# Two-layer hybrid decoder on one core: the two norms after each projection rewritten (gain at the eviction, squares from the bank, sums in groups), and a bank of its own for the last block

## The chip, the cores and the metric

The kernel runs on one core of a Trainium2 chip. The time is device microseconds of one launch. Inside the core five engines work side by side, each through its own queue in order: TensorE (PE in the profile: matrix products; PEld is its loading of weights), VectorE (DVE), ScalarE (ACT), GpSimd (POOL) and SyncE (SP, which here only issues DMAs). An instruction that waits holds up everything behind it in its engine's queue.

The kernel before takes 1241.69 us (median of 3 runs, 1241.63 to 1242.22).

## The reference, cut to what matters

Sequence 512 plus 16 learned tokens ahead of it (L = 528), model width D = 1024, two layers, all float32. The two lines that the change touches are the two sandwich norms:

```python
def _rmsnorm(x, w):
    y = x * lax.rsqrt(jnp.mean(x * x, axis=-1, keepdims=True) + EPS)
    return y * w

for i in range(DEPTH):                                       # 2
    m = mixer(_rmsnorm(h, pre_mix_norm[i]), ...)             # one projection, two attention-like groups, w_out
    h = h + _rmsnorm(m, post_mix_norm[i])
    f = conv_ffn(_rmsnorm(h, pre_ffn_norm[i]), ...)          # ffn_up, conv of width 3, gelu * gate, ffn_down
    h = h + _rmsnorm(f, post_ffn_norm[i])
return h[:, N_META:]
```

So after each of the four products (w_out and ffn_down, in each layer) comes a pair of norms: the product's result is normalised, weighted and added to h, and the new h is normalised and weighted for the next product. After the last ffn_down there is only the first of the pair.

## The kernel before

**Layout.** h and everything that enters a product lie with features on the 128 partitions and tokens along the free dimension: 8 tiles of 128 features, 528 tokens. Tokens go in two halves, 0 to 232 and 232 to 528 (in layer 1 the first half is 14 to 232, 218 tokens, behind the mixer). A float32 product is made of three 16-bit ones: weight and input are split into a high and a low 16-bit part, and `product_step` issues high·high (L469), high·low (L470: low part of the input) and low·high (L471: low part of the weight) for each tile. The weights come by DMA (SP queue) into `st`, ACT makes their high part (L120) and DVE the low part (L124), both into `unit`, just ahead of use.

**A product and its norms.** In `out_proj` (banks `po`) and `ffn_down` (`pd`) the first half's 8 output tiles are computed, then the second half's 8, then the next product (`pu` of ffn_up, or `pj` of the next mixer) starts with the first half's tokens. Each output bank is copied to `m` by ACT (L1106, L1298), squared by ACT from `m` (L430 or L433), and the square is added to `acc` (L435: in `out_proj` on GpSimd except for the last tile, in `ffn_down` on DVE). A half's `norms` (L438) then runs in steps that the kernel lays between the matmuls of what follows: `token_rstd` brings the sum over partitions (a matmul into `nst`, L419), a multiply-add on DVE (L402), the power -1/2 on GpSimd (L403), and spreads the result over all partitions by a matmul with a diagonal (`ndg` L647, `nbc` L643). Then for each of the 8 tiles: DVE m·gain·rstd into `tmp` (L448), GpSimd h += tmp (L450), ACT the square of h (L430/L433), DVE its addition (L435); a second `token_rstd`; and `scaled`: for each tile DVE h·gain·rstd into `tmp` (L656), ACT the high part (L407), DVE the low part (L408), into the input `xh` of the next product.

**What sets the order.** The kernel's beginning is ordered by hand; everything behind it is put in order by a scheduler that works from a cost table of its own, so an edit in one place can move instructions of other places in the queues.

**The seams.** The first half's norms run beside the second half's matmuls; the second half's norms run beside the next product's first matmuls. A seam is a place where PE turns to a half whose `xh` has only just been made: S1 (layer 0, w_out to ffn_up, about 279 us, needs the first half's), S2 (in layer 1's mixer, about 660 us, where its first-half projection is over and the second half's `xh`, from layer 0's ffn_down, is needed), S3 (layer 1, w_out to ffn_up, about 895 us, needs the first half's).

**The end.** `last_down` computes the last product with tokens on partitions, in four blocks of 128 tokens, by a scheme with fewer products than usual; the last block's last piece ("t4", block 3) is done in two column halves of 256, both into bank `pa[1]`. Each half is squared (L1392) and weighted (L1396) from the bank; then the last sum (L1397), the power (GpSimd, L1398), four results of 256 columns (L1401) and their DMAs (L1402).

Of the kernel before, what the change touches and what calls it, by code (L numbers as in the profile page):

```python
# [126 lines left out]
class Quarter:  # L127
# [22 lines left out]
    def fetch(self):  # L150
# [17 lines left out]
        nc.vector.scalar_tensor_tensor(out=self.unit[:, 1], in0=x, scalar=SW, in1=self.unit[:, 0], op0=ALU.mult, op1=ALU.subtract)  # L168
# [48 lines left out]
class Kern:  # L217
# [112 lines left out]
    def constants(self):  # L330
        nc, a, c = self.nc, self.a, self.const
        widths = (("h", KD * L), ("xroom", KD * L), ("ident", P), ("ones", P), ("mhalf", 10), ("par", NROW), ("pars", 48), ("cvec", 4 * 88), ("ss", 10), ("first", 10),
# [33 lines left out]
    def gains(self):  # L366
# [8 lines left out]
        nc.vector.tensor_scalar(out=self.pars[:, 16:], in0=pt[:, :32], scalar1=SX, scalar2=None, op0=ALU.mult)  # L375
# [61 lines left out]
    def norms(self, m, acc, xh, n0, n1, rpost, rpre):  # L437
# [6 lines left out]
        bc = out[0]  # L444
        acc2 = self.sm([P, WN], "acc", bufs=4)
        for k in range(KD):
            t = self.sm([P, WN], "tmp")
            nc.vector.scalar_tensor_tensor(out=t[:, :n], in0=m[:, k, n0:n1], scalar=self.par[:, rpost + k : rpost + k + 1],  # L448
                                           in1=bc[:, :n], op0=ALU.mult, op1=ALU.mult)
            nc.gpsimd.tensor_tensor(out=self.h[:, k, n0:n1], in0=self.h[:, k, n0:n1], in1=t[:, :n], op=ALU.add)  # L450
# [198 lines left out]

    def scaled(self, bc, xh, n0, n1, rpre):  # L650

        nc = self.nc
        n = n1 - n0
        for k in range(KD):
            t = self.sm([P, WN], "tmp")
            nc.vector.scalar_tensor_tensor(out=t[:, :n], in0=self.h[:, k, n0:n1], scalar=self.pars[:, rpre + k : rpre + k + 1],  # L656
                                           in1=bc[:, :n], op0=ALU.mult, op1=ALU.mult)
            self.split(xh[k], t[:, :n], n0, n1)
            if k % 2:
                yield  # L660
# [431 lines left out]
    def out_proj(self, l):  # L1092
# [7 lines left out]
        for n0, n1 in self.halves(l):  # L1100
            acc = self.sm([P, WN], "acc", bufs=4)
            for ct in range(KD):
# [3 lines left out]
                nc.scalar.activation(m[:, ct, n0:n1], ps[:, : n1 - n0], AF.Copy, scale=IW)  # L1106
                self.sumsq(acc, ct, m[:, ct, n0:n1], n1 - n0, ct == KD - 1)
                self.tick()
            gens.append(self.norms(m, acc, xh, n0, n1, R_POST + 8 * l, R_PREF + 8 * l))
# [4 lines left out]
    def input_sums(self):  # L1114

        nc = self.nc
        xf = cell(self.keep, [P, KD, L], F32, "xf", "xf", 1)
# [164 lines left out]
    def ffn_down(self, l, av):  # L1282
# [6 lines left out]
        for g in range(2):  # L1289
            for half, (n0, n1) in enumerate(hv):  # L1290
                for ct in range(4 * g, 4 * g + 4):
# [6 lines left out]
                    nc.scalar.activation(m[:, ct, n0:n1], ps[:, : n1 - n0], AF.Copy, scale=IAW)  # L1298
                    self.sumsq(accs[half], ct, m[:, ct, n0:n1], n1 - n0, True)
                    self.tick()  # L1300
                if g == 1:
                    gens.append(self.norms(m, accs[half], xh, n0, n1, R_POSTF + 8 * l, R_PRE + 8 * (l + 1)))
                    self.finish(gens[-1])
# [3 lines left out]
    def last_down(self, l, av):  # L1307
# [39 lines left out]
        def final(t):  # L1347
            s = self.sm([P, 2], "sst")[:, :1]
            nc.vector.tensor_tensor(out=s, in0=ss[:, 2 * t : 2 * t + 1], in1=ss[:, 2 * t + 1 : 2 * t + 2], op=ALU.add)
            r = self.rstd(s, 1, 1.0 / D, EPS)  # L1350
            for i in range(2):
# [122 lines left out]
```

## Time and profile before

| | |
|---|---|
| median of the runs | 1241.69 us |
| the profiled execution | 1243.79 us |
| its span, first to last recorded instruction | 1241.7 us |
| PE busy | 1221.0 us (98%) |
| DVE busy | 838.9 us (68%) |
| ACT busy | 667.5 us (54%) |
| GpSimd busy | 160.0 us (13%) |
| granted PE clock, mean | 0.998 |
| PE's share of the chain that ended last | 90% |

The profile is of one execution. A row of the timeline reads: start in us from the span's start, duration in us, engine, line, operation, output<-input, tile size, how many in a row ("x2"), and in brackets the engine's idle time before it with what ended it. Matmuls overlap in the pipe: the start of one to the start of the next is what a matmul costs, not its duration. A row of the windows reads: window and its length, then busy us (and instruction count) of PE, PEld, DVE, ACT and POOL, the granted PE clock as a share of full speed, the share of DMA time, and GB/s. In a group, "16 instructions" stands as x16, followed by the group's busy us and the mean ns of one.

### The profile page before, as it was taken

The page shows a single profiled execution, that of the slowest core. Times are in us where ns is not written, and L with a number is a line of the kernel's source. Part 1 is how long each engine was busy: PE and PEld are TensorE (multiplying, and loading weights), DVE is VectorE, ACT ScalarE, POOL GpSimd, SP SyncE. Part 2 cuts the span into 40 slices and gives each one's busy share as a digit, 9 for nine tenths or more (in the row PEclk, how much of TensorE's full clock was granted, in tenths as well). Part 3 has the DMA queues.
Part 4 walks back from the last instruction along what each step waited for, and adds up shares of the span by engine and source line. Part 5 has one row for each costly group of instructions (what it writes and reads, how often), then busy time and mean ns, then how long its engine had stood idle before and what let it go on. Part 6 is the DMA issues. An engine that isn't in the chain of part 4 may idle for free.

```text
span 1241.7 us, 26411 instructions
## 1 busy us (share of the span) xinstructions
PE 1221.0 (98%) x11079; PEld 1013.5 (82%) x11079; DVE 838.9 (68%) x1485; ACT 667.5 (54%) x1316; POOL 160.0 (13%) x205
## 2 busy tenths in 40 slices
PE   8999999999999999999999999999999999999997
PEld 7778888988888888988887788889798888886444
DVE  5677745467998777623465777443769768887686
ACT  5674445454776666523335654453648556664442
POOL 1012311153000000000220223011520000000001
PEclk9999999999999999999999999999999999999999
DMA  7932121131423333424243232212314333304461
GB/s 202 273 102 86 60 79 52 52 97 40 136 70 110 100 97 96 119 73 108 63 114 98 69 86 70 69 52 69 104 51 136 102 103 103 119 2 170 160 239 68
DMA packets 207275, 124.18 MB, mean 100 GB/s; under 512 B 6880, under 2 KB 194836, under 8 KB 207156
## 3 DMA queue, kind: packets, MB, share of 16 engines
q1 hardware_dynamic: 206708, 121.71, 33.7%
q8 instruction: 87, 1.43, 0.5%
q0 software_dynamic: 160, 0.52, 0.1%
q14 instruction: 32, 0.26, 0.1%
q10 hardware_dynamic: 288, 0.26, 0.1%
HBM read 120.38 MB, written 2.10 MB: 99 GB/s over the span
## 4 chain that ended last, share of the span: by engine, by line
PE 90%; ACT 3%; DVE 3%; issue 1%; POOL 1%; DMA 0%; SPq 0%; POOLq 0%; DVEq 0%; ACTq 0%
PE pu L470 11%; PE pu L471 11%; PE pu L469 11%; PE pl L1324 8%; PE pj L469 7%; PE pj L471 7%; PE pj L470 7%; PE pp L1145 3%; PE pd L470 3%; PE pd L471 3%; PE pd L469 3%; PE po L469 2%; PE po L471 2%; PE po L470 2%; PE o L776 1%
## 5 line engine op out<-in xcount | busy, mean ns | idle before, releaser
L470 PE MATMUL pu<-every,unit 128*128 128x296 f16 (+2 forms) x1248 | 341.2, 274 | 2.1 <-DVE every L408 2.1
L471 PE MATMUL pu<-every,unit 128*128 128x296 f16 (+2 forms) x1248 | 341.2, 274 | 0.0
L469 PE MATMUL pu<-every,unit 128*128 128x296 f16 (+2 forms) x1248 | 339.6, 274 | 0.7 <-ACT every L407 0.7
L471 PEld LDWEIGHTS <-unit 128*128 128x128 f16 x2700 | 264.4, 98 | 44.2 <-issue 3.8
L469 PEld LDWEIGHTS <-unit 128*128 128x128 f16 x2700 | 264.6, 98 | 43.9 <-issue 3.9
L470 PEld LDWEIGHTS <-unit 128*128 128x128 f16 x2700 | 264.8, 98 | 39.0 <-issue 0.6
L124 DVE SCALAR_TENSOR_TENSOR unit<-st,unit 128x1024 f16<-128x1024 f32 (+1 forms) x173 | 212.0, 1227 | 100.7 <-ACT unit L120 100.0
L471 PE MATMUL pj<-every,unit 128*128 128x296 f16 (+2 forms) x888 | 244.8, 276 | 0.9 <-DVE unit L124 0.9
L469 PE MATMUL pj<-every,unit 128*128 128x296 f16 (+2 forms) x888 | 245.1, 276 | 0.5 <-DVE room L933 0.5
L470 PE MATMUL pj<-every,unit 128*128 128x296 f16 (+2 forms) x888 | 244.9, 276 | 0.0
L120 ACT ACTIVATE unit<-st 128x1024 f16<-128x1024 f32 (+1 forms) x171 | 177.9, 1041 | 75.1 <-PE pu L471 21.2
L1201 ACT ACTIVATE u<-pu 128x296 f32<-128x296 f32 (+2 forms) x156 | 58.5, 378 | 72.6 <-PE pu L471 72.6
L435 DVE TENSOR_TENSOR acc<-acc,sq 128x296 f32<-128x296 f32 (+2 forms) x60 | 33.4, 558 | 77.6 <-ACT sq L433 75.7
L471 PE MATMUL pd<-av,unit 128*128 128x232 f16 (+1 forms) x308 | 84.7, 276 | 0.0
L470 PE MATMUL pd<-av,unit 128*128 128x232 f16 (+1 forms) x308 | 84.7, 276 | 0.0
L469 PE MATMUL pd<-av,unit 128*128 128x296 f16 (+1 forms) x308 | 84.5, 276 | 0.0
L403 POOL TENSOR_TENSOR every<-every 128x5 f32<-128x5 f32 (+6 forms) x31 | 38.1, 1229 | 295.7 <-DVE every L402 250.4
L1324 PE MATMUL pl<-unit,fk 128*128 128x512 f16 x330 | 71.4, 379 | 0.0
L1190 DVE SCALAR_TENSOR_TENSOR cg<-u,every,cg 128x527 f32<-128x527 f32 (+1 forms) x88 | 66.4, 754 | 5.0 <-ACT cg L1185 4.3
L471 PE MATMUL po<-merged,unit 128*128 128x296 f16 (+2 forms) x256 | 69.7, 274 | 0.0
L470 PE MATMUL po<-merged,unit 128*128 128x296 f16 (+2 forms) x256 | 69.7, 274 | 0.0
L469 PE MATMUL po<-merged,unit 128*128 128x296 f16 (+2 forms) x256 | 69.4, 274 | 0.0
(260 smaller groups left out, 1745.7 us busy)
## 6 DMA issues: line engine op xcount, KB each, us to landing
st<-in_ffn_up SPq DMA_DIRECT2D x78, 512.0 KB, 3.8
st<-in_w_in SPq DMA_DIRECT2D x56, 512.0 KB, 4.6
st<-in_ffn_down SPq DMA_DIRECT2D x46, 512.0 KB, 3.9
st<-in_w_out SPq DMA_DIRECT2D x16, 512.0 KB, 3.6
st<-in_ffn_up SPq DMA_DIRECT2D x20, 256.0 KB, 4.0
st<-in_ffn_down SPq DMA_DIRECT2D x8, 384.0 KB, 3.4
xt<-in_x SPq DMA_DIRECT2D x6, 256.0 KB, 6.2
w<-in_ffn_down SPq DMA_DIRECT2D x3, 512.0 KB, 4.3
```

What stands on the lines that cost most here:

```text
L120: self.kern.nc.scalar.activation(self.u[:, 0], self.st, AF.Copy, scale=SW)
L124: self.kern.nc.vector.scalar_tensor_tensor(out=self.u[:, 1, ks], in0=self.st[:, ks], scalar=SW, in1=self.u[:, 0, ks], op0=ALU.mult, op1=AL ...
L403: nc.gpsimd.tensor_tensor(out=r[:w, :n], in0=t[:w, :n], in1=self.mhalf[:w, :n], op=ALU.pow)
L435: eng.tensor_tensor(out=acc[:, :n], in0=acc[:, :n], in1=sq[:, :n], op=ALU.add)
L469: nc.tensor.matmul(ps[:, :n], w[:, 0, kk, :], x[:, 0, n0:n1], start=first, stop=False)
L470: nc.tensor.matmul(ps[:, :n], w[:, 0, kk, :], x[:, 1, n0:n1], start=False, stop=False)
L471: nc.tensor.matmul(ps[:, :n], w[:, 1, kk, :], x[:, 0, n0:n1], start=False, stop=last)
L776: nc.tensor.matmul(o[:, i, :], intra(i), vn(i), start=i == 0, stop=i == 0, skip_group_check=i > 0)
L1145: mm = lambda p, q, **kw: nc.tensor.matmul(ps, u[:, p, k, :], x[k][:, q], skip_group_check=more, **kw)
L1190: nc.vector.scalar_tensor_tensor(out=to, in0=u[:, max(lo, d) - d : L - d], scalar=self.cvec[:, ci(i) : ci(i) + 1], in1=to, op0=ALU.mult, o ...
L1201: nc.scalar.activation(u[:, n0:n1], ps[:, : n1 - n0], AF.Copy, scale=IXW)
L1324: mm = lambda x, w, **kw: nc.tensor.matmul(ps[:, cols], x, w[:, cols], skip_group_check=more, **kw)
```

## The change

`gained` takes the place of copy and `sumsq`: ACT's copy out of the bank now also multiplies with the norm weight (a scale per partition, from the widened table `pars`), and the square is taken from the bank itself, with a scalar scale. Who adds the squares is as before.

`norms` works in groups of tiles instead of tile by tile. First pass, groups of 4, 2 and 2: one DVE multiply of `m` by the spread rstd, one DVE addition to h (GpSimd before), one ACT square into `m`, and DVE additions that fold the group into `acc2`. Second pass, groups of 2, 2 and 4: one DVE multiply h·rstd into `m` (L468), then for each tile ACT the high part with the weight as scale (L471) and DVE the low part (L472). `scaled` is gone.

In `last_down` block 3's first 256 columns of "t4" go to a bank of their own, `pe`; what earlier pieces had left in `pa[1]` for those columns is copied out ahead (`done`, L1384) and added by DVE (L1399). The other blocks' results (L1356) come after the last weights' low part (L168) on DVE. The last sum is made before the second half is weighted, and the last row of results goes out in three pieces (512, 256, 256 columns).

```diff
-    def sumsq(self, acc, k, src, n, last):
+    def gained(self, ps, out, rpost, acc, k, n, scale, last):
+        nc.scalar.activation(out, ps, AF.Copy, scale=self.pars[:, rpost + k : rpost + k + 1])
         if k == 0:
-            nc.scalar.activation(acc[:, :n], src, AF.Square)
+            nc.scalar.activation(acc[:, :n], ps, AF.Square, scale=scale)
         else:
             sq = self.sm([P, WN], "sq", bufs=3)
-            nc.scalar.activation(sq[:, :n], src, AF.Square)
+            nc.scalar.activation(sq[:, :n], ps, AF.Square, scale=scale)
             eng = nc.vector if last else nc.gpsimd
             eng.tensor_tensor(out=acc[:, :n], in0=acc[:, :n], in1=sq[:, :n], op=ALU.add)
...
     def norms(...)
-        for k in range(KD):
-            t = self.sm([P, WN], "tmp")
-            nc.vector.scalar_tensor_tensor(out=t[:, :n], in0=m[:, k, n0:n1], scalar=self.par[:, rpost + k : rpost + k + 1],
-                                           in1=bc[:, :n], op0=ALU.mult, op1=ALU.mult)
-            nc.gpsimd.tensor_tensor(out=self.h[:, k, n0:n1], in0=self.h[:, k, n0:n1], in1=t[:, :n], op=ALU.add)
-            self.sumsq(acc2, k, self.h[:, k, n0:n1], n, True)
-            if k in (3, 6):
-                yield
-        yield
+        add = lambda to, x, y: nc.vector.tensor_tensor(out=to, in0=x, in1=y, op=ALU.add)
+        spread = lambda bc, k: bc[:, None, :n].to_broadcast([P, k, n])
+        for k0, k1 in ((0, 4), (4, 6), (6, 8)):
+            mk, hk = m[:, k0:k1, n0:n1], self.h[:, k0:k1, n0:n1]
+            nc.vector.tensor_tensor(out=mk, in0=mk, in1=spread(out[0], k1 - k0), op=ALU.mult)
+            add(hk, hk, mk)
+            nc.scalar.activation(mk, hk, AF.Square)
+            if k1 - k0 == 4:
+                add(mk[:, :2], mk[:, :2], mk[:, 2:])
+            if k0 == 0:
+                add(acc2[:, :n], mk[:, 0], mk[:, 1])
+            else:
+                add(mk[:, 0], mk[:, 0], mk[:, 1])
+                add(acc2[:, :n], acc2[:, :n], mk[:, 0])
+            yield
         yield from self.token_rstd(acc2, n0, n1, out)
-        yield from self.scaled(out[1], xh, n0, n1, rpre)
+        for k0, k1 in ((0, 2), (2, 4), (4, 8)):
+            mk = m[:, k0:k1, n0:n1]
+            nc.vector.tensor_tensor(out=mk, in0=self.h[:, k0:k1, n0:n1], in1=spread(out[1], k1 - k0), op=ALU.mult)
+            for k in range(k0, k1):
+                gain = self.pars[:, rpre + k : rpre + k + 1]
+                nc.scalar.activation(xh[k][:, 0, n0:n1], mk[:, k - k0], AF.Copy, scale=gain)
+                nc.vector.scalar_tensor_tensor(out=xh[k][:, 1, n0:n1], in0=mk[:, k - k0], scalar=gain, in1=xh[k][:, 0, n0:n1], op0=ALU.mult, op1=ALU.subtract)
+            yield
...
     def last_down(...)
+        done = self.g([P, 512], F32, "part")[:, :256]
+        nc.scalar.activation(done, pa[1][:, :256], AF.Copy, scale=IAW)
+        pe = self.mm([P, 512], "pl")
...
-        for i, cols in enumerate(half):
-            multiply(("t4", av["x22"], {1: pa[1]}, True), cols=cols)
...
+        multiply(("t4", av["x22"], {1: pe}, False), cols=first)
+        nc.vector.scalar_tensor_tensor(out=y[0][:, first], in0=pe[:, first], scalar=IAW, in1=done, op0=ALU.mult, op1=ALU.add)
...
+        multiply(("t4", av["x22"], {1: pa[1]}, True), cols=last)
...
+        for i, c0, n in ((1, 0, 512), (0, 0, 256), (0, 256, 256)):
```

How the queues read. A row is line, operation, output<-input, tile and the semaphores it waits for (DMAHW is a weight load that landed, Activation is ACT).

DVE at seam S1 before, from the low part of a weight unit (L124) that stands ahead of the second pass of the first half's norms:

```order
L124 SCALAR_TENSOR_TENSOR unit<-st,unit 128x1024 [waits DMAHW2_49,Activation_49]
L656 SCALAR_TENSOR_TENSOR tmp<-every,nbc 128x232 [waits PE_49]
L656 SCALAR_TENSOR_TENSOR tmp<-every,nbc 128x232 x3
L408 TENSOR_TENSOR every<-tmp,every 128x232 [waits Activation_49] x2
L656 SCALAR_TENSOR_TENSOR tmp<-every,nbc 128x232 [waits DVE_49]
L656 SCALAR_TENSOR_TENSOR tmp<-every,nbc 128x232
L124 SCALAR_TENSOR_TENSOR unit<-st,unit 128x1024 [waits DMAHW3_49,PE_49,Activation_49]
L408 TENSOR_TENSOR every<-tmp,every 128x232 [waits Activation_49] x2
```

The same stretch of DVE's queue after the change:

```order
L124 SCALAR_TENSOR_TENSOR unit<-st,unit 128x1024 [waits DMAHW2_49,Activation_49]
L468 TENSOR_TENSOR m<-every,nbc 128x2x232 [waits PE_49]
L468 TENSOR_TENSOR m<-every,nbc 128x2x232
L468 TENSOR_TENSOR m<-every,nbc 128x4x232 [waits DVE_49]
L440 TENSOR_TENSOR acc<-acc,sq 128x296 [waits Activation_49,Pool_49]
L124 SCALAR_TENSOR_TENSOR unit<-st,unit 128x1024 [waits DMAHW3_49,PE_49,Activation_49]
L472 SCALAR_TENSOR_TENSOR every<-m,every 128x232 [waits Activation_49] x5
```

The first low part of `xh` (L408 before, L472 after; `every` holds `xh`) stood behind four single-tile products; it now stands behind all eight tiles' products, the second half's last addition (L440) and a unit's low part. S3 has the same order with 218 tokens.

ACT at S1 before, from the copy of the second half's last bank but one:

```order
L1106 ACTIVATE m<-po 128x296
L433 ACTIVATE sq<-m 128x296 [waits Activation_49]
L407 ACTIVATE every<-tmp 128x232 [waits DVE_49] x2
L1106 ACTIVATE m<-po 128x296 [waits PE_49]
L120 ACTIVATE unit<-st 128x1024 [waits DMAHW3_49]
L407 ACTIVATE every<-tmp 128x232 [waits DVE_49] x2
L433 ACTIVATE sq<-m 128x296 [waits Activation_49]
```

And ACT there after the change, from the last bank:

```order
L433 ACTIVATE m<-po,every 128x296 [waits PE_49]
L438 ACTIVATE sq<-po 128x296
L120 ACTIVATE unit<-st 128x1024 [waits DMAHW3_49]
L471 ACTIVATE every<-m,every 128x232 [waits DVE_49,Activation_49]
L471 ACTIVATE every<-m,every 128x232
L471 ACTIVATE every<-m,every 128x232 [waits DVE_49]
```

The first two high parts (L407 before, L471 after) stood ahead of the last bank's copy; they now stand behind its copy, its square and a unit's high part.

DVE at S2 after the change, where the second half's `xh` of the next mixer is made:

```order
L468 TENSOR_TENSOR m<-every,nbc 128x2x296 [waits PE_49]
L468 TENSOR_TENSOR m<-every,nbc 128x2x296
L468 TENSOR_TENSOR m<-every,nbc 128x4x296 [waits DVE_49]
L896 TENSOR_SCALAR nl<-z,every 128x232 [waits Activation_49] x2
L472 SCALAR_TENSOR_TENSOR every<-m,every 128x296 [waits Activation_49] x8
```

Before, one L408 stood between the two `nl` rows, behind four single-tile products; now the first low part stands behind all eight tiles' products and both `nl` rows.

More of the change, by code (lines that the diff above doesn't have):

```diff
@@ L648, in diagonal @@
         return dg
[L650 to L660, printed above, removed]
     def plan(self):
@@ L1350, in final @@
             r = self.rstd(s, 1, 1.0 / D, EPS)
+            behind = self.blocks[-1].low
             for i in range(2):
-                nc.vector.scalar_tensor_tensor(out=ys[t][i], in0=ys[t][i], scalar=r[:, 0:1], in1=hps[t][i], op0=ALU.mult, op1=ALU.add)
+                one = nc.vector.scalar_tensor_tensor(out=ys[t][i], in0=ys[t][i], scalar=r[:, 0:1], in1=hps[t][i], op0=ALU.mult, op1=ALU.add)
+                self.tc.add_manual_dep(one.ins, behind.ins.name, mybir.DependencyInfo(mybir.DependencyClass.NoSync, mybir.DependencyReason.DATA), reason="last weights first")
                 nc.sync.dma_start(self.a["out"][0, P * t : P * (t + 1), 512 * i : 512 * (i + 1)], ys[t][i])
```

47 lines of the change are left out of this document (24 added, 23 removed).

## The prediction

> **What bounds the kernel now.** I read the page's first and fourth part, then the timeline where PE's idle time is.
>
> ```profile
> span 1241.7 us, 26411 instructions
> ...
> PE 1221.0 (98%) x11079; PEld 1013.5 (82%) x11079; DVE 838.9 (68%) x1485; ACT 667.5 (54%) x1316; POOL 160.0 (13%) x205
> ...
> PE 90%; ACT 3%; DVE 3%; issue 1%; POOL 1%; DMA 0%; SPq 0%; POOLq 0%; DVEq 0%; ACTq 0%
> ```
>
> PE is the bound: 98% busy, 90% of the chain. The change takes no matmul away, so it can act in four places only: where PE waits for norms (the three seams) and at the end. Taking work from GpSimd (160 us of 1241.7) is worth nothing where PE does not wait for it.
>
> Seam S1, timeline:
>
> ```profile
> 279.43 0.29 PE L471 MATMUL po<-merged,unit 128*128 128x296 f16 x1
> 279.50 1.54 DVE L656 SCALAR_TENSOR_TENSOR tmp<-every,nbc 128x232 f32<-128x232 f32 x4
> 280.43 0.46 PE L469 MATMUL pu<-every,unit 128*128 128x232 f16 x3 [0.71 <-ACT every L407]
> 280.65 0.40 ACT L1106 ACTIVATE m<-po 128x296 f32<-128x296 f32 x1
> 280.95 1.05 ACT L120 ACTIVATE unit<-st 128x1024 f16<-128x1024 f32 x1
> 281.41 0.26 PE L470 MATMUL pu<-every,unit 128*128 128x232 f16 x1 [0.52 <-DVE every L408]
> 282.32 1.21 DVE L124 SCALAR_TENSOR_TENSOR unit<-st,unit 128x1024 f16<-128x1024 f32 x1
> 282.89 0.46 PE L469 MATMUL pu<-every,unit 128*128 128x232 f16 x3
> 283.90 0.26 PE L470 MATMUL pu<-every,unit 128*128 128x232 f16 x1 [0.55 <-DVE every L408]
> ```
>
> Here a matmul of 296 columns takes 0.13 us from start to start, one of 232 takes 0.10. The last `po` would hand over at 279.56; `pu` starts at 280.43 (lost 0.87, for ACT's high part), the low·high rows at 281.41 instead of 280.73 (0.68) and 283.90 instead of 283.19 (0.71), both for DVE's low part. S1 costs 2.3 us.
>
> Seam S3 (0.09 us per matmul of 218):
>
> ```profile
> 894.74 0.29 PE L471 MATMUL po<-merged,unit 128*128 128x296 f16 x1
> 895.05 0.44 PE L469 MATMUL pu<-every,unit 128*128 128x218 f16 x3
> 896.08 0.25 PE L470 MATMUL pu<-every,unit 128*128 128x218 f16 x1 [0.59 <-DVE every L408]
> 898.32 0.44 PE L469 MATMUL pu<-every,unit 128*128 128x218 f16 x3
> 899.16 0.25 PE L470 MATMUL pu<-every,unit 128*128 128x218 f16 x1 [0.40 <-DVE every L408]
> ```
>
> 0.18 + 0.76 + 0.57: S3 costs 1.5 us.
>
> Seam S2, timeline and windows:
>
> ```profile
> 659.46 0.66 PE L886 MATMUL z<-gaT,every 32*128 32x232 f32 x4
> 659.57 1.82 DVE L656 SCALAR_TENSOR_TENSOR tmp<-every,nbc 128x296 f32<-128x296 f32 x4 [2.33 <-PE nbc L643]
> 660.99 0.29 PE L727 MATMUL pj<-every,unit 128*128 128x296 f16 x1 [0.87 <-ACT every L407]
> 661.12 0.41 PE L469 MATMUL pj<-every,unit 128*128 128x296 f16 x2
> 661.31 0.45 DVE L891 TENSOR_SCALAR nl<-z,every 128x232 f32<-128x232 f32 x1
> 661.68 0.46 DVE L408 TENSOR_TENSOR every<-tmp,every 128x296 f16<-128x296 f32 x1
> 662.19 0.41 PE L727 MATMUL pj<-every,unit 128*128 128x296 f16 x2 [0.66 <-DVE every L408]
> ```
>
> ```profile
> 659.29:662.70 3.41, 1.88 (x14) 1.14 (x13) 3.13 (x8) 2.15 (x6) 0.00 (x0) 0.99 0.00 0
> 662.70:666.11 3.41, 3.41 (x16) 2.13 (x14) 3.41 (x10) 2.01 (x5) 0.00 (x0) 0.51 0.02 5
> 666.11:669.52 3.41, 3.41 (x30) 2.64 (x28) 1.94 (x4) 0.68 (x1) 0.00 (x0) 1.00 0.00 0
> ```
>
> PE loses 0.87 and 0.83 (662.19 instead of 661.36), 1.7 us. Behind that wait the granted clock is 0.51 for 3.41 us: 16 matmuls instead of 30. That is half of 3.41, 1.7 us more. So at S2 the wait costs double.
>
> The end:
>
> ```profile
> 1230.44 0.69 DVE L1345 SCALAR_TENSOR_TENSOR yo<-pl,every 128x512 f32<-128x512 f32 x1 [1.89 <-ACT sqo L1344]
> 1231.18 0.42 DVE L1396 SCALAR_TENSOR_TENSOR yo<-pl,every 128x256 f32<-128x256 f32 x1
> 1231.65 3.76 PE L1324 MATMUL pl<-unit,m 128*128 128x256 f16 x33 [1.75 <-DVE every L402]
> 1232.38 1.41 DVE L1352 SCALAR_TENSOR_TENSOR yo<-yo,every,hp 128x512 f32<-128x512 f32 x2 [0.66 <-POOL every L403]
> 1235.50 0.38 ACT L1392 ACTIVATE sqo<-pl 128x256 f32<-128x256 f32 x1 [4.73 <-PE pl L1324]
> 1236.35 0.15 DVE L1397 SCALAR_TENSOR_TENSOR every<-every 128x1 f32<-128x1 f32 x1
> 1237.15 1.66 DVE L1401 SCALAR_TENSOR_TENSOR yo<-yo,every,hp 128x256 f32<-128x256 f32 x4 [0.65 <-POOL every L1398]
> ```
>
> PE waits 1.75 us. The row names L402; what holds the next matmuls is the reading of the bank that they write, L1396, which ends at 1231.60.
>
> **The change part by part.** Sizes first:
>
> ```profile
> L154 DVE TENSOR_TENSOR w<-w,st 128x1024 f32<-128x1024 f32 x9 | 11.0, 1219 | 0.0
> ...
> L408 DVE TENSOR_TENSOR every<-tmp,every 128x232 f16<-128x232 f32 x16 | 5.5, 391 | 0.1
> ...
> L450 POOL TENSOR_TENSOR every<-every,tmp 128x232 f32<-128x232 f32 x16 | 14.0, 909 | 6.3 <-DVE tmp L448 6.3
> ```
>
> Two DVE sizes give 0.828 us for 792 elements, 1.05 ns an element. Four L656 in a row take 1.54 us with the last at 0.45, so 0.36 from start to start, 0.12 over the elements. The trace has no wide multiply with a spread operand; I take the same two figures: 464 elements 0.61, 928 elements 1.09, 592 elements 0.74, 1184 elements 1.36. Grouping saves DVE only the 0.12 of each start.
>
> *First pass of the norms.* Eight GpSimd additions of 0.909 us (7.3 us) go, DVE gets them as wide ones (8 x 232 x 1.05 ns = 1.9 us). In a first half this runs beside the second half's matmuls and ends ahead of the seam before and after; in a second half it runs beside the next product. Cost 0. Without that cover the chain would be some 4 us shorter, at most what the seams lose today. The additions of squares in out_proj stay on GpSimd.
>
> *S1, second pass.* By the order of the queues, from the row at 279.50 on: DVE's wide products start at 279.50, 280.11, 280.72 and end at about 281.8. Then L440, which needs the last bank's square. ACT meanwhile: copy 279.76, square 280.10, L120 280.43, and by the 0.94 from L120 to the next instruction (rows before) the first high part at 281.37, so `pu` starts at about 281.8 instead of 280.43. DVE: L440 until 282.17, L124 (1.14 to the next start) until 283.31, first low part 0.40, so the first low row is at about 283.8. Between are only three high·high matmuls and three matmuls of sums (0.65 us). Lost: 283.8 - 279.56 - 0.65 = 3.6, against 2.3: **+1.3**. Behind it the low parts come each 0.36 us and PE takes three matmuls a tile, 0.30; the third wait of today, for L124, goes into the first. Low bound, if L440 were ready early and only ACT's copy, square, L120 and then L124 and one low part stood in the row: 279.72 + 0.36 + 0.30 + 0.97 + 1.14 + 0.45 = 282.9, +0.5. High bound: L124 at 1.83 us as in rows where GpSimd adds beside it,
>
> ```profile
> 277.75 1.83 DVE L124 SCALAR_TENSOR_TENSOR unit<-st,unit 128x1024 f16<-128x1024 f32 x1
> ```
>
> and a start half a microsecond later: +2.4.
>
> *S3.* The same with 218 tokens, but the order has `nbc` two matmuls ahead of `pu`, so DVE starts at about 894.8: products until 897.0, L440 897.4, L124 898.55, low part 898.9. Lost 898.9 - 894.87 - 0.64 = 3.4 against 1.5: **+1.9**; bounds by the same two cases +1.3 and +2.4.
>
> *S2.* DVE from 659.57: 0.74, 0.74, 1.36 to 662.41, two `nl` rows (0.37 each) to 663.15, low part 0.46: 663.6. Lost 663.6 - 660.12 - 0.36 = 3.1 against 1.7: **+1.4**, bounds +1.0 (the schedule's `nl` rows ready late would not help; products 0.4 shorter would) and +1.8.
>
> *Clock behind S1 and S3.* Today both run at full clock (window 280.40 to 283.82):
>
> ```profile
> 280.40:283.82 3.42, 2.40 (x21) 2.04 (x21) 3.42 (x9) 3.07 (x8) 0.00 (x0) 1.00 0.53 156
> 1229.30:1232.71 3.41, 1.66 (x14) 1.24 (x13) 1.61 (x7) 1.05 (x4) 0.54 (x1) 1.00 0.21 77
> ```
>
> After the change each has a stretch of about 4 us with 0.65 us of matmuls. A window of 3.41 us with 1.88 us busy was followed by half clock at S2, one with 1.66 us busy at the end was not. So the measure is not busy time alone in my windows; but a stretch that holds a third of that is nearer to the case that dropped. Between 0 and 1.7 us each; I take 1.0 each: **+2.0** (0 to 3.4). S2 keeps its drop.
>
> [...]
>
> *The end.* With a bank of its own PE doesn't wait: the last 33 matmuls end 1.9 us earlier. DVE then becomes the chain: L1348 from 1230.44 as today, y with `done` 0.42, sum and product of the first half, the two results of block 2 (1.41), then the second half's product (0.42) and the last sum at about 1234.7 instead of 1236.35; results as three pieces 1.5 instead of 1.66. **-1.8** (-1.2 if ACT's square of the first half, 0.38 and its read-out, holds DVE up, -2.3 if the two results come ahead of it).
>
> Sum: 1.3 + 1.9 + 1.4 + 2.0 - 1.8 = **+4.8**. The profiled execution took 1243.79 us (span 1241.7 and 2.1 around it) and would take 1248.6; the median of the runs is 2.1 below it, so I predict 1246.5 us. All bounds together: 0.5 + 1.3 + 1.0 + 0 - 2.3 = +0.5, and 2.4 + 2.4 + 1.8 + 3.4 - 1.2 = +8.8.
>
> **The rivals.**
>
> [...]
>
> *The groups finish ahead of the seam.* Faster. Then GpSimd's 0.909 us additions are what makes the second pass late at the seams; without them the whole first-half chain ends some 4 us earlier, if the order lets it, and the waits of S1, S3 and S2 with its half clock (2.3 + 1.5 + 1.7 + 1.7 = 7.2 us) go wholly or by half. For it: L450's long rows and the idle time ahead of them, 6.3 us waiting for L448. Against it: the order, where `nbc` stands at the last `po` matmuls and L440, L124 and L120 ahead of the split. With the end: 1241.69 - 3.6 - 1.8 = 1236.3, all of it 1232.7. It decides if the second pass starts more than 3 us before the last `po`.
>
> *The growth and the end cancel.* At the seams the low bounds, at the end the high one, no clock drop: +0.5, 1242.2 us. For it: PE's own matmuls between (sums, high rows) may be laid where my walk has a wait. This is also the case in which the change does little of what it says, since GpSimd keeps the squares' additions of out_proj.
>
> **How the numbers follow.** Chances: forecast 0.50, without the drop 0.18, cancelled 0.13, faster 0.19. About 0.2% (2.5 us) can be told from no change: below 1239.2 is faster, above 1244.2 slower. Forecast and the case without a drop are slower (0.66, a few hundredths of them fall inside the bound, as many of the cancelled case outside); same 0.15; faster 0.19. The upper end is the sum with nearly every upper bound, 1250; to leave out no more than 2 in 10, the lower end goes into the faster case, 1239.5. The likeliest case's own range is 1244 to 1250.
>
> **What would show it.** S1 and S3: `pu` starts 2 us after the last `po`, its first low·high row waits for DVE L472 until about 4 us after; windows behind with a granted clock near 0.5; S2's first low·high row at 4 us after `z` instead of 2.7. GpSimd without the rows of L450. At the end no idle time ahead of the last 33 matmuls, and the last sum about 1.2 us behind their end instead of 0.9. It would be wrong if the first L468 of S1 or S3 ended more than 2 us before the last `po`, if L472 were much shorter than 0.39 us, or if DVE at the end held PE in another way.

## The result: 0.75% slower

The changed kernel takes 1252.02 us (median of 5 runs, 1250.87 to 1254.05) against 1242.22 for the kernel before on the same chip: ratio 1.0075, 95% interval 1.0064 to 1.0086, so 9.8 us more, where 4.8 were forecast. On another chip it was 1253.02 against 1242.41, 1.0084 (1.0070 to 1.0097). The profiled execution took 1251.88 us.

The page of the changed kernel, first part:

```profile
span 1250.1 us, 26302 instructions
...
PE 1225.4 (98%) x11079; PEld 1016.4 (81%) x11079; DVE 834.5 (67%) x1439; ACT 667.4 (53%) x1287; POOL 118.4 (9%) x157
```

GpSimd lost 42 us of work and the kernel became no faster for it. PE's matmuls are the same 11079; its busy time grew by 4.4 us, which two more windows of half clock (below) account for in the main.

Where the 8.4 us of span lie: the start of the same matmul (same bank, same count) in the two profiles, as a ladder along the kernel. Between the steps its median over 20 us does not move by more than 0.03 us.

| stretch | step, us | forecast |
|---|---|---|
| first 12 us (other profiles lie 0.3 earlier to 1.6 later there) | +0.6 | 0 |
| S1 with the clock behind it | +2.5 | 1.3 + 1.0 |
| S2 | +2.0 | 1.4 |
| layer 1's mixer, 688 to 703 us | +1.3 | 0 |
| S3 with the clock behind it | +3.4 | 1.9 + 1.0 |
| the last block's wait of PE | -1.9 | -1.9 |
| behind the last matmul | +0.6 | +0.1 |

Seam S1 of the changed kernel, timeline:

```profile
279.64 0.29 PE L488 MATMUL po<-merged,unit 128*128 128x296 f16 x1
279.84 2.22 DVE L468 TENSOR_TENSOR m<-every,nbc 128x464 f32<-128x464 f32 x3 [0.25 <-PE nbc L660]
280.67 1.06 ACT L120 ACTIVATE unit<-st 128x1024 f16<-128x1024 f32 x1
281.97 0.46 DVE L440 TENSOR_TENSOR acc<-acc,sq 128x296 f32<-128x296 f32 x1
282.15 0.46 PE L486 MATMUL pu<-every,unit 128*128 128x232 f16 x3 [2.23 <-ACT every L471]
282.35 1.22 DVE L124 SCALAR_TENSOR_TENSOR unit<-st,unit 128x1024 f16<-128x1024 f32 x1
283.48 1.94 DVE L472 SCALAR_TENSOR_TENSOR every<-m,every 128x232 f16<-128x232 f32 x5
283.99 0.26 PE L487 MATMUL pu<-every,unit 128*128 128x232 f16 x1 [0.76 <-DVE every L472]
```

This is the walk of the prediction almost to the tenth: `pu` 2.5 us behind the last `po` (forecast 2.4), the first low·high row 4.35 us behind it (forecast 4.4), L440 and L124 ahead of the first L472. S3 is the same: `pu` 2.50 us behind `po`, the first low row 4.09.

```profile
901.07 0.29 PE L488 MATMUL po<-merged,unit 128*128 128x296 f16 x1
903.57 0.44 PE L486 MATMUL pu<-every,unit 128*128 128x218 f16 x3 [2.21 <-ACT every L471]
905.16 0.25 PE L487 MATMUL pu<-every,unit 128*128 128x218 f16 x1 [0.71 <-DVE every L472]
```

Windows of 3.41 us at the three seams of the changed kernel (the columns as in the table of the profile before):

```profile
281.52:284.93 3.41, 2.02 (x18) 1.69 (x18) 3.41 (x7) 3.23 (x9) 0.00 (x0) 0.98 0.39 116
284.93:288.34 3.41, 3.41 (x21) 2.62 (x19) 2.30 (x9) 0.00 (x0) 1.00 (x1) 0.52 0.51 144
288.34:291.75 3.41, 3.41 (x36) 3.37 (x34) 1.97 (x2) 0.45 (x2) 0.00 (x0) 1.00 0.00 0
664.10:667.51 3.41, 0.68 (x4) 0.39 (x4) 3.41 (x7) 3.31 (x8) 0.00 (x0) 0.94 0.01 2
667.51:670.92 3.41, 3.41 (x17) 2.07 (x16) 3.41 (x8) 1.54 (x3) 0.00 (x0) 0.56 0.03 7
902.70:906.11 3.41, 1.83 (x19) 1.84 (x20) 3.41 (x8) 3.38 (x9) 0.00 (x0) 0.99 0.42 126
906.11:909.52 3.41, 3.41 (x21) 2.83 (x19) 2.10 (x9) 0.00 (x0) 0.99 (x1) 0.51 0.51 146
```

Half clock now stands behind all three seams (0.52, 0.56 and 0.51 over 3.41 us in the rows above), 1.7 us each. At S3 the kernel before had 1.00 from 894.70 to 901.50 us. It seems to have half clock behind S2 in half of its executions only: of its 77 runs beside the experiments 39 have a mean granted clock of 0.999 and take 1241.7 to 1242.7 us, 38 have 0.996 to 0.998 and take 1243.2 to 1245.0. Its profile, with the window behind S2, was one of the latter; that this window is what parts the two groups is read from the mean clock and not from a second profile. So the profiles differ by 8.1 us and the medians by 9.8.

S2 and the layer 1 mixer, timeline, the changed kernel:

```profile
662.09 0.65 PE L891 MATMUL z<-gaT,every 32*128 32x232 f32 x2
662.67 0.69 PE L660 MATMUL nbc<-ndg,every 99*128 99x99 f32 x4
663.29 0.65 PE L891 MATMUL z<-gaT,every 32*128 32x232 f32 x2
663.40 2.75 DVE L468 TENSOR_TENSOR m<-every,nbc 128x592 f32<-128x592 f32 x3 [2.78 <-PE nbc L660]
665.13 0.29 PE L732 MATMUL pj<-every,unit 128*128 128x296 f16 x1 [1.19 <-ACT every L471]
666.07 0.82 DVE L896 TENSOR_SCALAR nl<-z,every 128x232 f32<-128x232 f32 x2
667.37 0.65 PE L732 MATMUL pj<-every,unit 128*128 128x296 f16 x2 [1.70 <-DVE every L472]
...
682.71 0.77 PE L891 MATMUL z<-gaT,every 32*128 32x296 f32 x4
692.57 1.16 PE L955 MATMUL d<-room 64*128 64x128 f32 x16
```

The same two places of the mixer in the kernel before:

```profile
674.64 0.77 PE L886 MATMUL z<-gaT,every 32*128 32x296 f32 x4
687.53 1.16 PE L950 MATMUL d<-room 64*128 64x128 f32 x16
```

At S2 the first low row comes 3.4 us behind the end of `z` (663.29 + 0.65), 3.5 as walked; but `z` and `nbc` now stand between each other. The step of 1.3 us behind it was not in the forecast: `z`, the second half's gate logits, stood 12.9 us ahead of `d` and now stands 9.9 us ahead. It moved a tile of the projection (3 us) later in PE's queue, and what waits for it came later too (tried below, with `z` held).

The end, the changed kernel:

```profile
1241.31 1.91 PE L1327 MATMUL pl<-unit,m 128*128 128x256 f16 x16
1242.83 1.40 DVE L1356 SCALAR_TENSOR_TENSOR yo<-yo,every,hp 128x512 f32<-128x512 f32 x2
1244.54 0.15 DVE L1408 SCALAR_TENSOR_TENSOR every<-every 128x1 f32<-128x1 f32 x1
1245.34 1.53 DVE L1413 SCALAR_TENSOR_TENSOR yo<-yo,every,hp 128x512 f32<-128x512 f32 x3 [0.65 <-POOL every L1409]
```

The wait of PE is gone. The last sum comes 1.32 us behind the last matmul's end (0.94 before), since the two results of block 2 are ahead of it on DVE, and so is the weighting of the second half (0.41 us), which the program has behind the sum.

### The profile page after: what moved, and what is told of

Its sections match the earlier page's. It is cut to its first block, busy times and chain, and to the rows that moved or that the text cites. A ratio compares the mean times of both kernels' runs of the same rounds, so it can differ in the third digit from the quotient of the medians.

```text
span 1250.1 us, 26302 instructions
## 1 busy us (share of the span) xinstructions
PE 1225.4 (98%) x11079; PEld 1016.4 (81%) x11079; DVE 834.5 (67%) x1439; ACT 667.4 (53%) x1287; POOL 118.4 (9%) x157
## 3 DMA queue, kind: packets, MB, share of 16 engines
q8 instruction: 87, 1.43, 0.5%
## 5 line engine op out<-in xcount | busy, mean ns | idle before, releaser
L124 DVE SCALAR_TENSOR_TENSOR unit<-st,unit 128x1024 f16<-128x1024 f32 (+1 forms) x173 | 209.7, 1213 | 106.0 <-ACT unit L120 105.2
L1194 DVE SCALAR_TENSOR_TENSOR ca<-u,every,ca 128x527 f32<-128x527 f32 (+1 forms) x88 | 66.5, 755 | 2.6 <-ACT ca L1189 1.6
```

The lines of the kernel that those rows point to most:

```text
L124: self.kern.nc.vector.scalar_tensor_tensor(out=self.u[:, 1, ks], in0=self.st[:, ks], scalar=SW, in1=self.u[:, 0, ks], op0=ALU.mult, op1=AL ...
L1194: nc.vector.scalar_tensor_tensor(out=to, in0=u[:, max(lo, d) - d : L - d], scalar=self.cvec[:, ci(i) : ci(i) + 1], in1=to, op0=ALU.mult, o ...
```

## The experiments

All medians are beside those of the kernel before on the same chip; ratios are to it. The median of the kernel before lies between 1242.19 and 1243.53 us on the four chips, with the share of its runs at a mean clock below 0.999, so ratios from different chips can be compared to about 1 us only.

**The end alone.** The kernel before with the changed `last_down`:

```diff
+        pe = self.mm([P, 512], "pl")
...
+        multiply(("t4", av["x22"], {1: pe}, False), cols=first)
```

> The kernel before with the changed last_down alone (own bank, earlier last sum, three result pieces); norms as before. The ladder of the two profiles (start of the same matmul in both) gives the last block 1.9 us less waiting of PE, of which 0.6 are given back behind the last matmul. Theory (the end is a gain of its own): 1.0 to 1.6 us below before. Rival (the gain is a by-product of the later norms, with DVE less crowded at the end): within 0.3 us of before.

1242.22 against 1243.53 us, 0.9985 (0.9975 to 0.9994): a gain of its own, 1.9 us by the ratio, 1.3 by the medians and by the profile's ladder. This half of the change is good.

**The additions to h back on GpSimd.**

```diff
-            add(hk, hk, mk)
+            nc.gpsimd.tensor_tensor(out=hk, in0=hk, in1=mk, op=ALU.add)
```

> The changed kernel with one thing undone: the additions to h of the norms' first pass run on GpSimd again (in the new wide groups). With it the queues at S1 and S3 come out in another order: two (S3: four) low parts of xh stand ahead of the last square's addition and of the weight unit's low part. Queue theory (what stands ahead of the first low part on DVE and ACT makes the seam long): S1 and S3 each 1.1 to 1.5 us shorter, and one or both drops of the clock behind them gone: 1244 to 1249. Rival one (the second pass starts late, since GpSimd's power -1/2 stands behind five additions of squares): GpSimd has more to do, the second pass starts later still, 1252 or more. Rival two (DVE has too much work): the seams shorten by the DVE time saved, about 2 us a half, wherever it lies, also behind the seams.

1250.38 us, 1.0049 (1.0034 to 1.0064). None of the three theories as written. In the profile, the shortest of the four runs (1248.44 us, mean clock 0.998 against 0.994 and 0.995), the queue theory's part at S1 came: PE waits 1.17 us once and no half clock follows S1 or S3. But the sum of the norms now holds PE earlier, in the middle of the second half:

```profile
274.43 0.57 PE L422 MATMUL nst<-every,acc 128*116 128x1 f32 x4 [1.52 <-DVE acc L450]
```

In layer 1 PE waits 1.43 us at the same place, and the ladder's step at S3 is 2.9 us without any half clock. So there is a third place where these norms can cost: `nst` itself, in PE's queue ahead of its data.

**The same instructions, another order.** In the second pass the last four tiles' product behind the first pair's low parts; at S1 and S3 the last bank's copy behind the first pair's high parts, and the addition of its square behind the second pair's low parts. `after` is an ordering between two instructions of one queue, without a wait (names shortened here and in the two diffs like it).

```diff
+            if k0 == 4:
+                self.after(one, low_of_second_tile)
...
+            if last and second half of out_proj:
+                self.after(copy, high_of_second_tile)
+                self.after(addition, low_of_fourth_tile)
```

> The changed kernel, the same instructions, only their order in the queues held: the product of the last four tiles of the second pass behind the first two low parts, and at S1 and S3 the last bank's copy, its square's addition behind the first pair. [...] Rival (the second pass starts late): S1 and S3 stay within 0.4 us, 1250 to 1252.

1246.26 us, 1.0022 (1.0013 to 1.0031): about 6 of the 9.8 us come back by order alone (5.8 by the medians, 6.6 by the ratios), and the rival is out. S1 in its timeline:

```profile
279.22 0.29 PE L502 MATMUL po<-merged,unit 128*128 128x296 f16 x1
279.43 1.19 DVE L476 TENSOR_TENSOR m<-every,nbc 128x464 f32<-128x464 f32 x2 [0.25 <-PE nbc L674]
281.04 0.46 PE L500 MATMUL pu<-every,unit 128*128 128x232 f16 x3 [1.52 <-ACT every L481]
281.79 0.82 DVE L482 SCALAR_TENSOR_TENSOR every<-m,every 128x232 f16<-128x232 f32 x2
282.29 0.26 PE L501 MATMUL pu<-every,unit 128*128 128x232 f16 x1 [0.79 <-DVE every L482]
```

The first low row is 3.07 us behind `po` instead of 4.35, the ladder's step at S1 is 0.0, and no half clock follows S1 or S3 in this execution (1.00 from 282.70 to 286.10 us and from 900.40 to 903.80). Its mean clock is 0.997, as in five of the ten runs; the other five have 0.996 and take 1.0 to 2.5 us more. The mixer's step of 1.3 us stays, and so does 1.2 us at S3.

**Matmuls of no use in the waits of S1 and S3.** The order of DVE and ACT at the seams is the changed kernel's.

```diff
+            if n0 == SPLIT:
+                fill = self.mm([P, WN], "po")
+                for i in range(18):
+                    nc.tensor.matmul(fill[:, : n1 - n0], self.merged[i % KD][:, 0, 64 : 64 + P], self.merged[i % KD][:, 0, n0:n1], start=True, stop=True)
```

> The changed kernel with 18 matmuls of no use (296 columns, about 2.3 us) behind the last w_out matmul of each layer, into a bank that nobody reads, so that PE is busy in the first half of the wait at S1 and S3; the queues of DVE and ACT at the seams stay as in the changed kernel. Theory (the half clock behind S1 and S3 comes from the low activity of PE in the wait): both windows of half clock go, 3.4 us less than the changed kernel, 1248 to 1249, and the waits stay. Rival (the drop has another cause): the windows stay, 1251.5 to 1252.5.

1248.62 us, 1.0040 (1.0027 to 1.0053), as the theory had it. Windows over S1:

```profile
279.50:282.90 3.40, 3.24 (x27) 2.43 (x26) 3.40 (x5) 3.37 (x8) 0.33 (x1) 1.00 0.54 155
282.90:286.30 3.40, 2.74 (x28) 2.70 (x28) 3.40 (x12) 1.41 (x4) 1.00 (x1) 1.00 0.51 149
286.30:289.70 3.40, 3.40 (x36) 3.36 (x35) 1.04 (x4) 0.36 (x1) 0.00 (x0) 1.00 0.04 10
```

With PE busy in the wait (3.24 of 3.40 us at S1; 3.36 at S3, from 899.50 to 902.90 us) the granted clock stayed at 1.00 there and in the 3.4 us behind, at both seams, and the ladder shows the waits bare: S1 0.8, S3 1.7 us. So of the 2.5 and 3.4 of the changed kernel 1.7 each are half clock, shown by taking it away.

**The eviction part alone.** Norm weight at the eviction, squares from the bank; passes tile by tile and the end as before.

```diff
-            nc.vector.scalar_tensor_tensor(out=t[:, :n], in0=m[:, k, n0:n1], scalar=gain, in1=bc[:, :n], op0=ALU.mult, op1=ALU.mult)
+            nc.vector.tensor_tensor(out=t[:, :n], in0=m[:, k, n0:n1], in1=bc[:, :n], op=ALU.mult)
```

> The kernel before with one part of the change: the norm weight at the eviction of w_out and ffn_down, the squares from the bank (the first pass then multiplies m with the spread rstd alone). Tile by tile as before, additions to h on GpSimd, last_down as before. In the queues at S1 and S3 two low parts stand ahead of the last square's addition and of two weight units. First-pass theory (the regrouped passes, not the eviction, make the seams long): S1, S2, S3 within 0.5 us each of before, total within 1.5 us of before. Rival (squares from the bank bunch up on GpSimd and hold up the power -1/2): the second pass starts 1 us later at S1 and S3, 2 to 4 us above before.

1250.87 against 1242.19 us, 1.0069 (1.0056 to 1.0081). Both theories fall. The seams are not long; the second pass is early. What costs is the last of these rows:

```profile
263.36 5.98 POOL L454 TENSOR_TENSOR every<-every,tmp 128x232 f32<-128x232 f32 x7
266.33 4.78 DVE L461 TENSOR_TENSOR acc<-acc,sq 128x232 f32<-128x232 f32 x7
271.16 0.94 PE L422 MATMUL nst<-every,acc 128*116 128x1 f32 x4 [4.69 <-DVE acc L461]
```

The scheduler laid the second `nst` at 266.2 us in PE's queue, among the second half's matmuls; its sum, behind GpSimd's additions of 0.85 us each, is ready at 271.2. The same `nst` in the kernel before:

```profile
272.98 0.47 PE L419 MATMUL nst<-every,acc 128*116 128x1 f32 x4
```

PE stands 4.7 us in layer 0 and 3.7 in layer 1; the `po` matmuls behind `nst` in the queue, which take nothing from it, start again at 271.95. Half clock comes with both (mean clock 0.994): in layer 0 those `po` matmuls start 0.25 us apart from 272.15 to 275.61 us, and 0.13 apart ahead of the wait. That the scheduler's own costs made the new multiply shorter and so pulled `nst` forward is inferred, not tried.

**The second pass as before, in the changed kernel.**

```diff
-        for k0, k1 in ((0, 2), (2, 4), (4, 8)):
...
+        yield from self.scaled(out[1], xh, n0, n1, rpre)
```

> The changed kernel with the second pass undone alone: tile by tile, weight and rstd in one DVE operation into four small buffers, the split from there. The last square's addition and a weight unit's low part still stand ahead of the first low part at S1 and S3. First-pass theory: the seams stay long; four products of 1.54 us take the place of three of 2.2, so S1 and S3 are 0.7 us shorter each, S2 1 us: 1246 to 1250. Rival (the wide groups of the second pass are the cause): S1, S2, S3 go back to before, 1240.5 to 1242.5 with the gain at the end.

1247.35 us, 1.0040 (1.0024 to 1.0056): inside the first theory's range, above the rival's. Undoing the wide groups of the second pass brings back 4.7 us by the medians, which is a part and not all; the run on the order got 5.8 back with groups as wide. In the profile (1250.57 us, the longest of the four runs) PE's wait at S1 is now mostly for L440, the second half's sum, which `nst` needs and which stands ahead of `pu` in PE's queue.

**All additions of squares on DVE**, so that GpSimd has the power alone:

```diff
-            eng = nc.vector if last else nc.gpsimd
-            eng.tensor_tensor(out=acc[:, :n], in0=acc[:, :n], in1=sq[:, :n], op=ALU.add)
+            nc.vector.tensor_tensor(out=acc[:, :n], in0=acc[:, :n], in1=sq[:, :n], op=ALU.add)
```

> The changed kernel with all additions of squares on DVE, none on GpSimd, whose queue then holds the power -1/2 alone. Late-start theory (GpSimd's power behind five additions makes the second pass late, and that is the seam's length): the second pass starts 1.4 us earlier at S1 and S3, and the first low row comes 1.4 us earlier. Queue theory: it can come at most 0.7 us earlier, since the last bank's copy and square, the weight unit's high and low part still stand ahead and cannot start before the last w_out matmul; 1248 to 1252, clock drops where they are.

1253.82 us, 1.0091 (1.0076 to 1.0107): no gain, and above the 1248 to 1252 of the queue theory. The second pass does not start earlier, since `nbc` stands where it stood in PE's queue, and the first low row comes 4.8 us behind the first `nbc`, as in the changed kernel. GpSimd's queue is out as a cause.

**The eviction part and the end.** Both parts of the two kernels above.

> The eviction part and the new last_down together, passes as before. If the parts add, this is the eviction part alone less 1.3 to 1.9 us, 1 to 3 us below before, and the fastest so far. Rival (the parts do not add, since the end depends on how DVE comes out of the norms): the eviction part alone within 0.5 us.

1249.22 us, 1.0053 (1.0040 to 1.0065), the eviction part less 2.0 us by the ratios: the end's gain adds to what stands ahead of it. That sum was expected 1 to 3 us below before and is 6.6 above by the ratio, since the eviction part alone was so long.

**That kernel with `nst` held.**

```diff
+                if n0 == SPLIT and ct == 6:
+                    self.after(second_nst_of_first_half, first_matmul_of_this_tile)
```

> The eviction part and the new last_down, with one thing held: the second sums over the partitions (nst) of the first half's norms stand in PE's queue behind the first matmul of the second half's seventh tile of w_out, near where they stood before, and not 6 us earlier. Theory (that kernel lost its time because PE stood 4 to 5 us at these matmuls for a sum that DVE and GpSimd had not finished, and the half clock behind it): 7 to 9 us less than without the hold, 1 to 3 us below before. Rival (the chain of the norms is late by itself, so the wait moves to the seam): 2 us less at most.

1243.65 against 1242.41 us, 1.0010 (1.0002 to 1.0019): 5.3 us back for one ordering. That is less than the 7 to 9 expected; `nst` no longer waits, but `nbc` does (1.56 us at 277 us), and behind the mixer's wait of 2.6 us at 687 us, where `z` stands 9.9 us ahead of `d` as in the changed kernel, there is a window of half clock (mean clock of this execution 0.997). With the end's gain in it this is still above before, so the eviction part costs some 3 us even so.

**The seam order and `z` held.**

```diff
+        if l:
+            self.after(first_matmul_of_fifth_tile, last_z)
```

> The changed kernel with the order held at the seams as in the run on the seam order, and in layer 1's mixer the second half's gate matmuls (z) held ahead of the fifth tile of the projection, where they stood before; in the changed kernel they stand a tile (3 us) later in PE's queue. Theory (the 1.1 to 1.3 us lost at 688 to 703 us come from that place alone, since the chain z, gate, decay is the longest of the mixer): 1.1 us less than the seam order alone, 1.0 to 2.0 us above before. Rival (they come from ACT and DVE being behind after the seam): no change.

1245.62 us, 1.0024 (1.0015 to 1.0034), by the ratio the same total as the seam order alone, as the rival had it. The theory's place is confirmed all the same, its price hidden: `z` stands at 676.48 and `d` at 689.36, 12.9 us as before, and the ladder's step over the mixer went from +1.3 to -0.5. But in this profile half clock follows S1 and S3 again (mean clock 0.994 against 0.997), with the same two waits there, 1.81 and 1.05 us from start to start, as in the seam order's profile, which had none. Runs with equal mean clock (0.996) take 1244.9 to 1245.7 us here and 1246.8 to 1247.6 there.

**The changed kernel again.**

> The changed kernel as it is, beside the others on one chip, for a second profile. Theory (the ladder is fixed by the order of the queues, and the windows of half clock come with the waits): S1 +2.5, S2 +2, the mixer +1.3, S3 +3.4 against the profile before, each within 0.7, and half clock behind all three seams. Rival (the half clock is chance): it is missing behind one of them, which is then 1.7 shorter.

1253.02 us, 1.0084 (1.0070 to 1.0097). The steps are 2.4, 3.2, 1.8 and 4.2 us: S1 as in the first profile, the other three up to 1.2 longer, at S2 and S3 more than the 0.7 that the theory left. The granted clock is 0.50 from 665.20 to 672.02 us at S2 and from 904.13 to 910.96 at S3, 6.8 us each and twice as long as in the first profile, and for 3.4 us in the mixer; the mean clock is 0.991 against 0.995. PE's waits at S1 and S2 and its first wait at S3 are the same to 0.02 us; what varies from execution to execution is the clock.

**The end, and fillers at S2 of the kernel before.** 8 matmuls, 0.8 us.

> The kernel before with the new last_down, and 8 matmuls of no use (232 columns, 0.8 us) in the wait of S2, behind the first half's last projection. Theory (activity in the wait holds the clock): the window of half clock behind S2 goes, 1.7 us less than with the new last_down alone, 3 to 4 us below before. [...]

1240.59 us, the lowest median here, 0.9986 (0.9977 to 0.9995). The profile's window behind S2 is gone (the ladder falls by 2.0 there), but the ratio is that of the end alone: by the mean clock the window is there in only some executions of the kernel before, so its removal is worth less than 1.7 us and is not told apart. This profile has a window of half clock elsewhere, at 11.7 us (mean clock 0.997; seven of the eleven runs have 0.999).

**Fillers at all three seams of the changed kernel.**

> The changed kernel with matmuls of no use in the waits of all three seams: 18 (296 columns) at S1 and S3, 12 (232 columns) at S2. Theory (of the 9.8 to 10.6 us, three windows of 1.7 us are half clock behind the seams, and the rest is waits): 5 us less than the changed kernel, 4.5 to 6 us above before, and no window of half clock in the profile behind the start. Rival (the second wait of 2 us at S2, which no filler reaches, drops the clock by itself): 3.4 us less only, with the window behind S2 left.

1243.51 against 1243.30 us, 1.0004 (0.9995 to 1.0013): about 9 us less than without, nearly twice the theory's 5. No window of half clock is left ahead of the last matmul (mean clock 0.999), worth 5.1 us. The rest is order: with the fillers there the `nl` rows came out behind the first pair's low parts at S2, and `z` back at 12.9 us ahead of `d`; the ladder's steps at S2 and in the mixer fell from the 2.5 and 1.3 us of the run with fillers at S1 and S3 alone to -0.8 and -0.5. So this run shows what order and clock cost together, and not the clock alone.

**Orders held and fillers.**

> The kernel with the order held at the seams and z held, with 10 matmuls of no use at S1 and S3 and 8 at S2. Theory (what that kernel still loses is windows of half clock that its waits of 1.8 and 1 us bring in some executions): 3 to 4 us less than without fillers, 0 to 1.5 us below before, in line with the gain at the end less what the waits at S1 and S3 still cost. Rival (it is waits that the order left): within 1 us of the kernel without fillers, 2 to 3 us above before.

1241.54 us, 0.9988 (0.9979 to 0.9997): 4.5 us less than without fillers by the ratios (3 to 4 were expected), 1.5 below before. All eleven runs have a mean clock of 0.998 or 0.999. The new norms, ordered well and with the clock held, come within 1 us of the old ones with the new end.

## Why the prediction was wrong in size

**Direction and mechanism held.** The forecast was slower, by longer waits at the three seams and half clock behind them, less a gain at the end. Each of these was measured, S1's order of events within 0.2 us. The run that changed order alone brings 5.8 to 6.6 of the 9.8 us back, and the run with fillers shows the clock's part at S1 and S3. The chance of 0.66 went to the right side. The rival that the groups finish ahead of the seam is out: `nbc` stands at the last `po`, and the second pass starts 0.2 us behind it. The case without the drop is out by the three windows, and the one in which growth and end cancel by the time.

**Sizes.** Forecast +4.8, measured +9.8:

- *The clock term*, 2.0 us, is the mis-sized one: it measured 5.1 by the profile's three windows. I took 1.0 for each of S1 and S3, between 0 and 1.7; it was 1.7 each, and the run with fillers takes both away. And "S2 keeps its drop" made S2 free: the profile had that window, but by the mean clock half of the executions of the kernel before do not, nor, by its time, does the median run here (1242.22 us), while the changed kernel's S2 has it in both profiles. So the third window is in the medians and not in the difference of the profiles. The forecast took 2.1 us off the profiled time to reach the median, and most of these 2.1 are, by the mean clock, that window.
- *Left out: 1.3 us in layer 1's mixer.* The prediction let the change act "in four places only", the three seams and the end, and put all other stages at nothing. No instruction in the mixer was edited; a small matmul was laid one tile later. I compared the queues of DVE and ACT at the seams and not PE's queue behind them.
- *S2's wait*: 2.0 instead of 1.4, above its bound of 1.8; `z` now also stands among the `nbc` matmuls. S1's and S3's waits are 0.8 and 1.7 instead of 1.3 and 1.9. At S1 the walk itself came out; but the kernel before also lost 0.4 us at `nbc` ahead of the last `po` (from one `po` to the next across the `nbc` 0.95 us, now 0.57), which the 2.3 us of the prediction did not hold and which is gone.
- *The end*: -1.3 instead of -1.8. PE's wait went wholly; behind it the last sum and the last outputs gave back 0.6 instead of 0.1.

Sum of the misses: 3.1 + 1.3 + 0.6 - 0.7 + 0.5 = 4.8, of 5.0 missing. The upper bound of 8.8 was a sum of bounds on listed terms, and the time lies above it because the mixer was not on the list and the window behind S2 was counted on both sides.

**The clock and the waits.** At S1 the window ahead of the drop has 2.02 of 3.41 us busy, at S3 1.83, at S2 0.68: half clock came here behind windows that were 41% to 80% idle. It did not always: in the seam order's profile no drop follows a stretch with less work than at S1 or S3, 1.08 of 3.40 us, 68% idle.

```profile
279.30:282.70 3.40, 1.08 (x10) 0.71 (x9) 3.24 (x6) 3.15 (x7) 0.55 (x1) 1.00 0.54 158
282.70:286.10 3.40, 3.40 (x38) 3.36 (x36) 3.40 (x8) 1.74 (x5) 0.00 (x0) 1.00 0.53 154
```

Two profiles have the same waits there (1.81 and 1.05 us), one with the drop (mean clock 0.994) and one without (0.997). So where no matmuls of no use stand in it, neither the length of the wait nor PE's busy share in it tells here whether the clock drops; what does is not shown.

**Still open.** Why the scheduler laid `nst`, `nbc` and `z` as it did was not tried; the runs show only that the places moved and what each costs. How many windows each of the changed kernel's executions has can be read from the mean clock alone: the profile with three at the seams has 0.995, the second one, with twice that length of half clock, 0.991, and the other runs have 0.991 to 0.994. What decides in which executions the kernel before has the window behind S2 is open too.

## What to carry to other kernels

Where a scheduler places small matmuls from another engine's results among large ones, read TensorE's own queue after every edit, far behind the edit too: a wait that no instruction's duration explains can stand there (4.7 us at `nst` in the eviction part alone). A wait of about 2 us on a busy TensorE cost 1.7 us more in clock here, in some executions twice that. Matmuls of no use in the wait removed it in the profiles (granted clock 1.00 from 279.50 to 289.70 us at S1); an order that brings the first operand earlier did so in some executions only (with the seam order five of ten have a mean clock of 0.997, five 0.996). Take the clock from several executions and not from one profile. Widening vector operations saved little (at S1 eight tiles took 2.22 us in three operations, where four single ones took 1.54) and lost more by an order in which the first consumer stands behind the last producer.

## What the hardware showed that was not expected

Half clock came with waits of 1.8 and 1 us in one execution (mean clock 0.994) and not in another of nearly the same kernel (0.997). At the seams it lasted 3.4 us at a time, or 6.8 in some (665.20 to 672.02 us in the second profile of the changed kernel). With 0.8 us of matmuls in the wait at S2 both profiles held full clock there (mean clock 0.997, with the window at 11.7 us, and 0.999); as half of the executions before seem to hold it without them, that 0.8 us is enough is not shown.
